# Delta rule's key-times-value product in the attention's rotating PSUM bank; first three second-layer weight casts of the feed-forward in traced order

## The chip, the cores and the metric

One core of one Trainium2 chip runs the kernel in one launch. The metric is device time in microseconds (us): the median of three timed runs of the kernel before is 1024.48 us (1024.39 to 1025.72).

## The reference

One layer of a hybrid encoder step, in float32, for two groups that share the weights: a prompt of 512 tokens and a sample of 64 tokens that has caches and a recurrent state. Width 1024, 4 heads in each attention, feed-forward width 4096.

```python
# h = x + W_out [ GDN_group(n) ; DiffAttn_group(n) ],  n = rmsnorm(x)
# h = h + MemCrossAttn(rmsnorm(h), memory K/V)
# h = h + W2 relu(W1 rmsnorm(h))^2
def step(S, xs):                                   # gated delta rule, one chunk
    u_c, w_c, qk_c, qg_c, kd_c, gl_c = xs
    vn = u_c - jnp.einsum('bhcd,bhde->bhce', w_c, S)
    o = jnp.einsum('bhcd,bhde->bhce', qg_c, S) + jnp.einsum('bhij,bhje->bhie', qk_c, vn)
    S = S * gl_c[..., None, None] + jnp.einsum('bhcd,bhce->bhde', kd_c, vn)
    return S, o
oa = _rmsnorm(oa, p['gdn_norm']) * jax.nn.silu(z)  # output of the delta rule, normalized and gated
h = h + jnp.square(jax.nn.relu(hn @ p['w_ff1'])) @ p['w_ff2']
```

The change touches the last product of `step`, kd times vn, that makes the next state, and the weights of `w_ff2`. The outputs include the new state of both groups.

## The kernel before

**Numbers.** Large products run in a split form: weight and activation are each cut into a high part (a cast on ScalarE, ACT) and a rest (a subtraction on VectorE, DVE), and three matmuls, high-high, high-low and low-high, add up in PSUM. In the program's names `wh`, `wl`, `w2h`, `w2l` are the parts of weights. The delta rule's own small products and transposes run on float32 tiles of 128 by 128.

**Stages.** Input projections come first (to about 120 us), then the gated delta rule over the prompt in four chunks of 128 tokens (to about 275 us), then the difference attention of four heads with the sample's delta rule woven in, the memory attention, and from about 600 us the feed-forward in eight groups of 512 hidden columns. Projections of later stages (tiles `pr`) are issued between the delta rule's steps and fill TensorE (PE) while the other engines work.

**One chunk of the delta rule.** `gdn_prep` (the triangle's solve by doubling, tiles `g`, products with `Dt`, `X`, `Y`, mask products `B` of L725) runs one chunk ahead of `gdn_scan` (L782). `gdn_scan` makes, in this order: keys times state; `vn` (L801); the output `bo`, which adds queries times state and KQ times `vn` in a PSUM bank; kd times `vn` in a bank of its own; the state update `next_state` (L760), for the first chunk a copy on ACT, later four instructions on DVE (L766, one per head); and then `normed` (L769) on `bo`: a square on ACT (L773), a reduction (L774), three small operations (L775, L776, L778) around a power on GpSimd (L208), and the scaling into `on` (L780). `on` is transposed on PE (L113) and gated (L814). `gdn_scan_sample` (L817) does the same for the sample, from a state that DMA loads (L877) into the buffer of the prompt's state, after that has been written out (L872).

**Banks.** PSUM's eight banks are handed out by tag: `BANKS = dict(pr=3, ba=2, g0=1, g1=1, gs=1)` (L75). A tag with one buffer makes each new tile wait until the last reader of the one before is done. All products of `gdn_scan` take "gs", one after the other. The tag "ba" turns over two buffers and serves the attention: transposes of keys and values (results copied at L932, L937, L940, and keys sent out at L938 and L941), and in the feed-forward the sums of `ff1_pair`. Tiles of one tag take their buffers in the order in which the program was written.

**Order.** Each engine runs its instructions in a fixed order. A scheduler sets it when the kernel is built, from dependences, the order in which the program was traced, and priorities: what is issued under `tc.high_priority()` is placed as early as it can be. DMAs of weights and states are issued on SP's queue, in order too.

**Feed-forward, the first split group.** `ff1_pair` makes two blocks of 128 hidden columns by seven products of twelve matmuls, numbered 1 to 7, in the order 1, 5, 6, 2, 7, 3, 4. `x`, `y`, `z` are the banks "ba", "gs" and "g1" that they add into; `keep` (L1364 to L1367, copy at L1366) saves the sum in a bank before the next product adds to it: product 6 adds to `x` after the first `keep`, product 7 after the third, product 3 to `z` after the second. `weights2` (L1334) loads a block of `w_ff2` (256 KB, DMA at L1336) and `split` casts it (L1330 on ACT, L1331 on DVE) with high priority. In the loop over groups g = 1 to 7 and blocks m = 0 to 7, `ff1_pair` runs at m = 0 and m = 4, and `project` with block m of the second layer at each m (L1519).

Of the kernel before, what the change touches and what calls it, by code (L numbers as in the profile page):

```python
# [15 lines left out]
P = 128  # L16
# [21 lines left out]
def hybrid_layer_kernel(  # L38
# [61 lines left out]
    def bank(tag="ba"):  # L100
        return ps.tile([P, 512], F32, tag=tag, name=nm(tag), bufs=BANKS[tag])
# [145 lines left out]
    w2 = w_in[0]  # L247
# [246 lines left out]
    for a0, n in HALVES:  # L494
        b = bank("pr")
# [286 lines left out]
    def gdn_scan(c, L, q, S):  # L782

        (_, kb), (cq, qb) = (blocks(typ, c, L) for typ in (1, 0))
        wide = [P, 4, P]

        def each(f):
            b = bank("gs")
            for h in range(H):
                f(b[:, h * P : (h + 1) * P], h)  # L790
            return v4(b, 4)

        if S is None:
            r = q["vb"]
        else:
            b = each(lambda o, h: mm(o, kb(h), S[:, h, :]))
            r = sb("r", 1)
            V.tensor_tensor(r, q["vb"], b, ALU.subtract)
        b = each(lambda o, h: mm(o, q["X"][:, h, :], r[:, h, :]))
        vn = sb("vn", 1)  # L800
        V.tensor_tensor(vn, b, q["brk"].unsqueeze(2).to_broadcast(wide), ALU.mult)  # L801

        def out(o, h):
            if S is not None:
                mm(o, qb(h), S[:, h, :], stop=False)
            mm(o, q["KQ"][:, h, :], vn[:, h, :], start=S is None)

        bo = each(out)
        b = each(lambda o, h: mm(o, q["kd"][:, h, :], vn[:, h, :]))
        S = next_state(c, S, b)  # L810
        on = sb("on", 1)
        normed(q, 4, [(slice(0, P), bo)], on)
        bt = each(lambda o, h: tr(o, on[:, h, :]))
        V.scalar_tensor_tensor(cq, bt, gn, zs[:, :, L], ALU.mult, ALU.mult)  # L814
        return S

    def gdn_scan_sample(q, S):  # L817
# [6 lines left out]
        def pairs(b):  # L824
            return b.rearrange("p (b i v) -> p b i v", b=2, i=2)

        def each(f, n=2 * P):
            b = bank("gs")
            for i in range(nb):
                f(b[:, i * n : (i + 1) * n], i)  # L830
            return b
# [17 lines left out]
            mm(o, q["KQ"][:, i, :], vw[:, i, :], start=False)  # L849

        bo = pairs(each(out))
        S = next_state(c, S, v4(each(lambda o, i: mm(o, q["kd"][:, i, :], vw[:, i, :])), 4))
        nc.sync.dma_start(o_gdn_s[0, 0].rearrange("h k v -> k h v"), S)
        yield
        on4 = sb("on", 1)
# [467 lines left out]
    odd = lambda: ft("f1", [P, 2, 4, T], 1, F32R)  # L1323
    rB = ft("rB", [P, T], 1)

    def split(src, tag, bufs, dma=False):
        shape = list(src.shape)
        wh, wl = (ft(tag + x, shape, bufs, F32R) for x in "hl")
        with tc.high_priority():
            A.copy(wh, src)  # L1330
            V.tensor_tensor(wl, src, wh.bitcast(F32), ALU.subtract)  # L1331
        return wh, wl

    def weights2(w, c0):  # L1334
        raw = ft("r2", [P, 4, P], 3)
        nc.sync.dma_start(raw, w[:, c0 : c0 + P].rearrange("(k p) n -> p k n", p=P))  # L1336
        return split(raw, "w2", 3)

    NG = 8

# [173 lines left out]
    for g in range(1, NG):  # L1514
        nxt = odd() if g % 2 else pair(5, F32R)
        for m in range(KT):
            if m % 4 == 0:
                ff1_pair(2 * g + m // 4, nxt)
            project(weights2(w_ff2[0, (g - 1) * 512 : g * 512, :], m * P), (pend,), add_group(g - 1, m), kt=4)  # L1519
            if g == 2:  # L1520
                with tc.issue_after(nc.cur_bb.bb.instructions[-1]):
                    square_block(m)
            if g == 3 and m == 0:
                norm_rows()
            if g == NG - 1:
                merge(V, m, slice(0, T if m < 4 else 256))
                if m >= 4:
                    last_weights(2 * m - 8)
        pend = nxt
# [57 lines left out]
```

## Time and profile before

| what | value |
|---|---|
| median of three timed runs | 1024.48 us (1024.39 to 1025.72) |
| profiled execution, its own time | 1023.02 us |
| its span in the trace | 1021.3 us |
| mean granted clock of TensorE | 0.998 |
| ScalarE busy | 535.1 us (52%) |
| HBM read and written | 88.88 MB, 87 GB/s over the span |

Times in the trace are microseconds from the span's start. A row of the timeline has the start, the time, the engine, the line of the kernel, the operation, the tile written and the tiles read, how many instructions the row joins, and in brackets the idle time before it with what ended it. PE is matmuls, PEld the weight loads that overlap them. A product of float32 tiles shows twice as many matmuls in the trace as the program issues.

### The profile page before, as it was taken

The page shows a single profiled execution, that of the slowest core. Times are in us where ns is not written, and L with a number is a line of the kernel's source. Part 1 is how long each engine was busy: PE and PEld are TensorE (multiplying, and loading weights), DVE is VectorE, ACT ScalarE, POOL GpSimd, SP SyncE. Part 2 cuts the span into 40 slices and gives each one's busy share as a digit, 9 for nine tenths or more (in the row PEclk, how much of TensorE's full clock was granted, in tenths as well). Part 3 has the DMA queues.
Part 4 walks back from the last instruction along what each step waited for, and adds up shares of the span by engine and source line. Part 5 has one row for each costly group of instructions (what it writes and reads, how often), then busy time and mean ns, then how long its engine had stood idle before and what let it go on. Part 6 is the DMA issues. An engine that isn't in the chain of part 4 may idle for free.

```text
span 1021.3 us, 17302 instructions
## 1 busy us (share of the span) xinstructions
PE 999.5 (98%) x6630; PEld 917.5 (90%) x6630; DVE 705.8 (69%) x1529; ACT 535.1 (52%) x1170; POOL 66.9 (7%) x131
## 2 busy tenths in 40 slices
PE   9999999999999999999999999999999999999986
PEld 7989899998888877899998998999999999999976
DVE  6666785776567676666666787757766677777893
ACT  6654664343364675544454657655545554555434
POOL 3441010100000000000000000000000000000030
PEclk9999999999999999999999999999999999999999
DMA  7432320100312255624121233422222222222102
GB/s 203 131 109 71 105 85 21 44 21 22 105 47 81 71 194 185 186 83 120 47 63 42 63 114 93 125 83 83 83 83 84 83 83 83 83 83 85 61 21 93
DMA packets 121254, 89.99 MB, mean 88 GB/s; under 512 B 5506, under 2 KB 112128, under 8 KB 120660
## 3 DMA queue, kind: packets, MB, share of 16 engines
q1 hardware_dynamic: 120804, 88.24, 29.4%
q8 instruction: 52, 0.85, 0.4%
q10 hardware_dynamic: 368, 0.66, 0.2%
q14 instruction: 30, 0.25, 0.1%
HBM read 79.14 MB, written 9.74 MB: 87 GB/s over the span
## 4 chain that ended last, share of the span: by engine, by line
PE 83%; DVE 5%; issue 3%; ACT 2%; POOL 2%; DMA 1%; POOLq 0%; ACTq 0%; DVEq 0%; SPq 0%
PE pr L107 48%; PE g L107 14%; PE ba L107 10%; PE gs L107 7%; PE ba L113 2%; PE g L113 2%; DVE u L1439 1%; DMA r<-in_w_ff_dram 1%; DVE wl L162 0%; POOL tg L208 0%; DMA S<-in_state_gdn_dram 0%; DVE p L457 0%; DMA out_dram<-S 0%; POOL X L604 0%; DVE on L780 0%
## 5 line engine op out<-in xcount | busy, mean ns | idle before, releaser
L107 PE MATMUL pr<-u,wh 128*128 128x320 f32 (+2 forms) x1240 | 326.9, 342 | 1.1 <-DVE p L323 1.0
L107 PE MATMUL pr<-u,wl 128*128 128x256 f32 (+1 forms) x816 | 228.3, 304 | 0.0
L107 PEld LDWEIGHTS pr<-u,wh 128*128 128x128 f32 x1240 | 211.4, 188 | 17.1 <-DVE p L323 1.3
L107 PEld LDWEIGHTS pr<-u,wl 128*128 128x128 f32 x816 | 149.9, 189 | 3.5 <-issue 0.7
L162 DVE TENSOR_TENSOR wl<-raw,wh 128x1024 fp32r<-128x1024 f32 x65 | 79.5, 1223 | 43.5 <-ACT wh L161 41.7
L161 ACT CAST wh<-raw 128x1024 fp32r<-128x1024 f32 x65 | 68.2, 1049 | 72.4 <-PE pr L107 55.5
L107 PE MATMUL pr<-u,w2h 128*128 128x320 f32 (+1 forms) x384 | 98.5, 340 | 1.4 <-DVE u L1415 0.7
L1330 ACT CAST w2h<-r 128x512 fp32r<-128x512 f32 x56 | 34.7, 620 | 92.3 <-PE pr L107 89.2
L107 PE MATMUL pr<-f,w2h 128*128 128x320 f32 (+1 forms) x288 | 73.8, 340 | 0.0
L107 PEld LDWEIGHTS pr<-u,w2h 128*128 128x128 f32 x384 | 65.0, 188 | 6.9 <-DVE u L1415 1.0
L107 PE MATMUL pr<-u,w2l 128*128 128x256 f32 (+1 forms) x256 | 65.2, 295 | 0.0
L107 PE MATMUL ba<-u,wl 128*128 128x288 f32 x360 | 53.0, 296 | 2.1 <-ACT keep L1366 2.1
L1415 DVE TENSOR_TENSOR u<-u,pr 128x256 f32<-128x256 f32 x96 | 42.9, 449 | 16.4 <-PE pr L107 15.6
L107 PEld LDWEIGHTS pr<-f,w2h 128*128 128x128 f32 x288 | 48.7, 188 | 4.2 <-issue 1.2
L107 PEld LDWEIGHTS ba<-u,wl 128*128 128x128 f32 x360 | 49.2, 188 | 3.0 <-ACT keep L1366 3.0
L107 PE MATMUL pr<-f,w2l 128*128 128x256 f32 (+1 forms) x192 | 48.8, 295 | 0.0
L107 PEld LDWEIGHTS pr<-u,w2l 128*128 128x128 f32 x256 | 46.9, 188 | 1.5
L1331 DVE TENSOR_TENSOR w2l<-r,w2h 128x512 fp32r<-128x512 f32 x56 | 39.2, 701 | 11.7 <-ACT w2h L1330 11.4
L107 PE MATMUL pr<-wh,u 128*128 128x512 f32 x128 | 41.2, 401 | 0.0
L1423 POOL TENSOR_TENSOR u<-u,rB 128x320 f32<-128x320 f32 x4 | 3.7, 921 | 497.4 <-ACT u L1438 492.8
L107 PEld LDWEIGHTS pr<-f,w2l 128*128 128x128 f32 x192 | 35.2, 188 | 1.1
L1375 ACT ACTIVATE c<-c 128x288 f32<-128x288 f32 x48 | 21.0, 442 | 28.5 <-DVE c L1374 28.5
(505 smaller groups left out, 2091.5 us busy)
## 6 DMA issues: line engine op xcount, KB each, us to landing
raw<-in_w_ff_dram SPq DMA_DIRECT2D x36, 512.0 KB
raw<-in_w_in_dram SPq DMA_DIRECT2D x28, 512.0 KB
r<-in_w_ff_dram SPq DMA_DIRECT2D x56, 256.0 KB
raw<-in_w_mem_k_dram SPq DMA_DIRECT2D x8, 512.0 KB
raw<-in_w_mem_v_dram SPq DMA_DIRECT2D x8, 512.0 KB
raw<-in_w_out_dram SPq DMA_DIRECT2D x8, 512.0 KB
raw<-in_w_mem_q_dram SPq DMA_DIRECT2D x8, 512.0 KB
raw<-in_w_mem_o_dram SPq DMA_DIRECT2D x8, 512.0 KB
```

The costliest lines, as they stand in the source:

```text
L107: i = nc.tensor.matmul(out, lhsT, rhs, start=start, stop=stop, skip_group_check=skip_group_check)
L113: i = nc.tensor.transpose(out, in_, ident[:n, :n])
L161: A.copy(wh, raw)
L162: V.tensor_tensor(wl, raw, wh.bitcast(F32), ALU.subtract)
L1330: A.copy(wh, src)
L1331: V.tensor_tensor(wl, src, wh.bitcast(F32), ALU.subtract)
L1375: A.activation(c, c, AF.Relu)
L1415: V.tensor_tensor(am, am, b, ALU.add)
L1423: eng.tensor_tensor(am, am, rB[:, n], ALU.mult)
L1439: V.tensor_tensor(lo, src, hi.bitcast(F32), ALU.subtract)
```

## The change

The inner function `each` of both scans takes the tag of its bank. Only kd times `vn` is given another, "ba" in place of "gs"; what is computed stays the same. In the feed-forward `split` and `weights2` take a flag `urgent` in place of an unused one; the casts of the blocks m = 0, 1, 2 of group g = 1 are issued without high priority, all others as before.

```diff
--- before.py
+++ after.py
@@ -784,8 +784,8 @@
         (_, kb), (cq, qb) = (blocks(typ, c, L) for typ in (1, 0))
         wide = [P, 4, P]
 
-        def each(f):
-            b = bank("gs")
+        def each(f, tag="gs"):
+            b = bank(tag)
             for h in range(H):
                 f(b[:, h * P : (h + 1) * P], h)
             return v4(b, 4)
@@ -806,7 +806,7 @@
             mm(o, q["KQ"][:, h, :], vn[:, h, :], start=S is None)
 
         bo = each(out)
-        b = each(lambda o, h: mm(o, q["kd"][:, h, :], vn[:, h, :]))
+        b = each(lambda o, h: mm(o, q["kd"][:, h, :], vn[:, h, :]), "ba")
         S = next_state(c, S, b)
         on = sb("on", 1)
         normed(q, 4, [(slice(0, P), bo)], on)
@@ -824,8 +824,8 @@
         def pairs(b):
             return b.rearrange("p (b i v) -> p b i v", b=2, i=2)
 
-        def each(f, n=2 * P):
-            b = bank("gs")
+        def each(f, n=2 * P, tag="gs"):
+            b = bank(tag)
             for i in range(nb):
                 f(b[:, i * n : (i + 1) * n], i)
             return b
@@ -849,7 +849,7 @@
             mm(o, q["KQ"][:, i, :], vw[:, i, :], start=False)
 
         bo = pairs(each(out))
-        S = next_state(c, S, v4(each(lambda o, i: mm(o, q["kd"][:, i, :], vw[:, i, :])), 4))
+        S = next_state(c, S, v4(each(lambda o, i: mm(o, q["kd"][:, i, :], vw[:, i, :]), tag="ba"), 4))
         nc.sync.dma_start(o_gdn_s[0, 0].rearrange("h k v -> k h v"), S)
         yield
         on4 = sb("on", 1)
@@ -1323,18 +1323,18 @@
     odd = lambda: ft("f1", [P, 2, 4, T], 1, F32R)
     rB = ft("rB", [P, T], 1)
 
-    def split(src, tag, bufs, dma=False):
+    def split(src, tag, bufs, urgent):
         shape = list(src.shape)
         wh, wl = (ft(tag + x, shape, bufs, F32R) for x in "hl")
-        with tc.high_priority():
+        with tc.high_priority() if urgent else ExitStack():
             A.copy(wh, src)
             V.tensor_tensor(wl, src, wh.bitcast(F32), ALU.subtract)
         return wh, wl
 
-    def weights2(w, c0):
+    def weights2(w, c0, urgent):
         raw = ft("r2", [P, 4, P], 3)
         nc.sync.dma_start(raw, w[:, c0 : c0 + P].rearrange("(k p) n -> p k n", p=P))
-        return split(raw, "w2", 3)
+        return split(raw, "w2", 3, urgent)
 
     NG = 8
 
@@ -1516,7 +1516,7 @@
         for m in range(KT):
             if m % 4 == 0:
                 ff1_pair(2 * g + m // 4, nxt)
-            project(weights2(w_ff2[0, (g - 1) * 512 : g * 512, :], m * P), (pend,), add_group(g - 1, m), kt=4)
+            project(weights2(w_ff2[0, (g - 1) * 512 : g * 512, :], m * P, g > 1 or m > 2), (pend,), add_group(g - 1, m), kt=4)
             if g == 2:
                 with tc.issue_after(nc.cur_bb.bb.instructions[-1]):
                     square_block(m)
```

The products stay as many as before; the order on the engines is another, from the first chunk of the delta rule to the end of the difference attention, and again in the first feed-forward group.

First place: TensorE in the third chunk (chunk 2), from the last matmul of the output `bo` (tile `gs_2438`) on. `vn_2436` times `kd_1987` is the product in question, `on_2456` the normalized output, `g_...` the next chunk's triangle, `pr_...` a projection. Before:

```order
L107 MATMUL gs_2438<-vn_2436,KQ_2031 128x128
L113 MATMUL g_392_2342<-ident,Dt_380_2296 128x128 x4
L113 MATMUL g_423_2474<-ident,u_75 128x128 x2
L107 MATMUL pr_3089<-u_94,wh_3064 128x320 x2
L107 MATMUL pr_3089<-u_94,wl_3065 128x320 x2
L107 MATMUL g_395_2351<-Dt_380_2296,B_394_2349 128x128 x4
L107 MATMUL pr_3089<-u_94,wh_3064 128x320 x2
L107 MATMUL pr_3122<-u_93,wh_3118 128x512
L107 MATMUL pr_3122<-u_93,wl_3119 128x256
L107 MATMUL gs_2447<-vn_2436,kd_1987 128x128
L107 MATMUL g_396_2357<-Y_393_2348,X_2295 128x128 x4
L107 MATMUL gs_2447<-vn_2436,kd_1987 128x128 x3
```

And now, from the row after the output's last matmul:

```order
L113 MATMUL g_392_2342<-ident,Dt_380_2296 128x128 x4
L107 MATMUL ba_2447<-vn_2436,kd_1987 128x128 x4
L107 MATMUL g_395_2351<-Dt_380_2296,B_394_2349 128x128 x4
L113 MATMUL g_423_2474<-ident,u_75 128x128 x2
L107 MATMUL pr_3068<-u_94,wh_3064 128x512
L107 MATMUL pr_3068<-u_94,wl_3065 128x256 x2
L107 MATMUL g_396_2357<-Y_393_2348,X_2295 128x128 x4
L107 MATMUL pr_3068<-u_94,wh_3064 128x512
L107 MATMUL pr_3089<-u_93,wh_3064 128x320 x2
L113 MATMUL g_426_2482<-ident,u_78 128x128 x2
L107 MATMUL pr_3089<-u_93,wl_3065 128x320
L113 MATMUL gs_2466<-ident,on_2456 128x128 x4
```

The product stands right behind the output in a "ba" tile, and the transposes of `on` stand about where the product stood.

The same chunk on VectorE, from the reduction L774 to the scaling L780 and behind it. Before:

```order
L774 TENSOR_REDUCE tg_2457<-on_2456 128x4
L775 TENSOR_TENSOR tg_2457<-tg_2457,tg_2035 128x4
L776 TENSOR_SCALAR tg_2457<-tg_2457 128x4
L778 TENSOR_TENSOR tg_2458<-tg_2458,tg_1980 128x4
L780 TENSOR_TENSOR on_2456<-gs_2438,tg_2458 128x512
L725 SCALAR_TENSOR_TENSOR B_404_2391<-lev,At_371_2267 128x512
L918 COPY qz_2680<-pr_3089 64x320
L162 TENSOR_TENSOR wl_3185<-raw_3182,wh_3184 128x1024
L741 TENSOR_TENSOR Dt_380_2296<-Dt_380_2296,g_396_2357 128x512
L766 SCALAR_TENSOR_TENSOR S_1962<-S_1962,egl,gs_2447 128x128 x4
```

And now:

```order
L774 TENSOR_REDUCE tg_2457<-on_2456 128x4
L775 TENSOR_TENSOR tg_2457<-tg_2457,tg_2035 128x4
L766 SCALAR_TENSOR_TENSOR S_1962<-S_1962,egl,ba_2447 128x128 x3
L725 SCALAR_TENSOR_TENSOR B_404_2391<-lev,At_371_2267 128x512
L766 SCALAR_TENSOR_TENSOR S_1962<-S_1962,egl,ba_2447 128x128
L776 TENSOR_SCALAR tg_2457<-tg_2457 128x4
L678 TENSOR_TENSOR kd_2477<-g_423_2474,kdc_1194 128x256
L778 TENSOR_TENSOR tg_2458<-tg_2458,tg_1980 128x4
L780 TENSOR_TENSOR on_2456<-gs_2438,tg_2458 128x512
```

The four updates of the state (L766), a mask product (L725) and a scaling of the prepared keys (L678) moved ahead of the normalization's last steps.

Second place: TensorE in the fourth chunk. `u_78` holds keys of the attention's first head, whose transposes go to "ba" tiles. Before, around kd times `vn`:

```order
L107 MATMUL gs_2628<-vn_2617,kd_2233 128x128 x3
L107 MATMUL g_462_2586<-Y_459_2579,X_2525 128x128 x2
L107 MATMUL gs_2628<-vn_2617,kd_2233 128x128
L107 MATMUL pr_3188<-u_93,wl_3185 128x256
L107 MATMUL pr_3188<-u_94,wh_3184 128x512
L107 MATMUL pr_3188<-u_94,wl_3185 128x256
L113 MATMUL g_463_2590<-ident,Dt_441_2526 128x128 x2
L107 MATMUL pr_3188<-u_94,wh_3184 128x512
L107 MATMUL pr_3188<-u_94,wl_3185 128x256
L107 MATMUL pr_3188<-u_94,wh_3184 128x512
L107 MATMUL g_466_2597<-Dt_441_2526,B_465_2595 128x128 x2
L113 MATMUL gs_2647<-ident,on_2637 128x128 x4
```

And now, from that product on:

```order
L107 MATMUL ba_2628<-vn_2617,kd_2233 128x128 x2
L107 MATMUL g_461_2582<-Dt_441_2526,B_460_2580 128x128 x2
L107 MATMUL ba_2628<-vn_2617,kd_2233 128x128 x2
L113 MATMUL ba_2765<-ident,u_78 128x128
L107 MATMUL g_462_2586<-Y_459_2579,X_2525 128x128 x2
L113 MATMUL ba_2765<-ident,u_78 128x128
L107 MATMUL pr_3122<-u_94,wl_3119 128x256
L107 MATMUL pr_3122<-u_94,wh_3118 128x512
L107 MATMUL pr_3147<-u_93,wh_3118 128x320
L113 MATMUL ba_2797<-ident,u_78 128x128
L113 MATMUL g_463_2590<-ident,Dt_441_2526 128x128 x2
L113 MATMUL ba_2797<-ident,u_78 128x128
```

The product moved ahead, next to the triangle's products, and the transposes of the first head's keys (`ba_2765`, `ba_2797`) moved behind it; they had been issued in earlier chunks. SP's queue, with the write of the prompt's state (L872) and the load of the sample's (L877), before:

```order
L157 DMA raw_3807<-in_w_in_dram 128x8x128
L872 DMA out_dram<-S_1962 128x4x128
L1140 DMA B_926_5048<-in_cache_mem_v_dram 128x512
L949 DMA u_76<-in_cache_diff_v_dram 128x2x512
L877 DMA S_2663<-in_state_gdn_dram 128x4x128
```

And now:

```order
L938 DMA out_dram<-p_493_2768 128x2x128
L872 DMA out_dram<-S_1962 128x4x128
L938 DMA out_dram<-p_496_2801 128x2x128
L941 DMA out_dram<-p_496_2801 64x128
L951 DMA p_509_2880<-in_cache_diff_k_dram 128x512
L877 DMA S_2663<-in_state_gdn_dram 128x4x128
```

Three transfers of the attention (L938, L941, L951) stand between the write and the load, in place of two (L1140, L949).

Third place: ScalarE in the first split pair of feed-forward group 1. `keep_6776`, `keep_6790` and `keep_6804` are the three copies, `w2h_7084` and `w2h_7115` second-layer blocks. Before:

```order
L1229 CAST wh_6881<-raw_6757 128x512
L1330 CAST w2h_7084<-r_1263_7082 128x512
L1380 CAST u_6616<-c_6730 128x288
L1330 CAST w2h_7115<-r_1268_7113 128x512
L1229 CAST wh_6884<-s_1225_6879 128x512
L1366 COPY keep_6776<-ba_6761 128x288
L1366 COPY keep_6790<-g_1216_6763 128x288
L1366 COPY keep_6804<-ba_6761 128x288
L1375 ACTIVATE c_6818<-c_6818 128x288
```

And now:

```order
L1229 CAST wh_6881<-raw_6757 128x512
L1380 CAST u_6616<-c_6730 128x288
L1366 COPY keep_6776<-ba_6761 128x288
L1330 CAST w2h_7084<-r_1263_7082 128x512
L1229 CAST wh_6884<-s_1225_6879 128x512
L1366 COPY keep_6790<-g_1216_6763 128x288
L1330 CAST w2h_7115<-r_1268_7113 128x512
L1366 COPY keep_6804<-ba_6761 128x288
L1375 ACTIVATE c_6818<-c_6818 128x288
```

Each cast of a second-layer block moved back behind a `keep` that it stood ahead of.

## The prediction

> **What bounds the kernel now.** I read the page's busy shares first, then the list of waits of TensorE (PE), then stretches of 25 us, then the timeline at the two places that the diff touches.
>
> ```profile
> span 1021.3 us, 17302 instructions
> PE 999.5 (98%) x6630; PEld 917.5 (90%) x6630; DVE 705.8 (69%) x1529; ACT 535.1 (52%) x1170; POOL 66.9 (7%) x131
> ```
>
> PE is busy for 999.5 of 1021.3 us, so only some 22 us of idle exist, start and tail included. An edit that leaves PE's work alone, as this one does, gains or loses through PE's waits. Those that bear on the change (engine, tile and line, what was waited for; us in total, times, longest):
>
> ```profile
> PE gs L107 <- DVE on L780: 2.1, 4, 0.9
> PE ba L107 <- ACT keep L1366: 2.1, 1, 2.1
> PE gs L107 <- DMA S<-in_state_gdn_dram: 0.5, 1, 0.5
> ```
>
> The first is the product kd·vn waiting for the one "gs" bank, which the normalization of the output (L780) still reads. The second is the sixth of the seven products of a pair in the first split feed-forward group. The third is the sample's state, loaded over DMA into the buffer that the prompt's state had.
>
> ```profile
> 225.00:250.00 25.00, 23.97 (x189) 21.59 (x189) 13.90 (x34) 9.10 (x19) 2.02 (x2) 1.00 0.09 22
> 250.00:275.00 25.00, 24.66 (x185) 21.77 (x185) 16.17 (x40) 9.37 (x21) 1.01 (x1) 1.00 0.25 68
> 650.00:675.00 25.00, 24.97 (x171) 23.86 (x170) 14.94 (x26) 16.39 (x39) 0.00 (x0) 1.00 0.31 91
> ```
>
> The columns are length, then busy us of PE, PEld, DVE, ACT, POOL, the granted clock, DMA. In the delta rule (first two rows) PE still has a microsecond of idle; in the feed-forward (third) it has none, so a microsecond won just before that stage is kept to the end, with nothing behind to take it back.
>
> **Part B, the casts.** PE and then ACT in the pair concerned:
>
> ```profile
> 622.92 1.75 PE L107 MATMUL g<-u,wh 128*128 128x288 f32 x12
> 624.51 1.61 PE L107 MATMUL gs<-u,w 128*128 128x288 f32 x11
> 628.22 1.86 PE L107 MATMUL ba<-u,wl 128*128 128x288 f32 x12 [2.10 <-ACT keep L1366]
> 633.72 1.87 PE L107 MATMUL ba<-u,w 128*128 128x288 f32 x12
> ```
> ```profile
> 623.25 0.60 ACT L1229 CAST wh<-raw 128x512 fp32r<-128x512 f32 x1
> 625.86 0.62 ACT L1330 CAST w2h<-r 128x512 fp32r<-128x512 f32 x1 [2.01 <-DMA r<-in_w_ff_dram]
> 626.38 0.42 ACT L1380 CAST u<-c 128x288 fp32r<-128x288 f32 x1
> 626.73 0.62 ACT L1330 CAST w2h<-r 128x512 fp32r<-128x512 f32 x1
> 627.25 0.61 ACT L1229 CAST wh<-s 128x512 fp32r<-128x512 f32 x1
> 627.77 0.39 ACT L1366 COPY keep<-ba 128x288 f32<-128x288 f32 x1
> 628.06 0.40 ACT L1366 COPY keep<-g 128x288 f32<-128x288 f32 x1
> ```
>
> The in-order ScalarE stands at the cast of a second-layer block whose DMA has not landed (2.01 us idle), and the copy `keep` that frees product 6's bank is queued behind it. Twelve matmuls take 624.51 − 622.92 = 1.59 us, 0.1325 each. The trace has 49 matmuls from 624.51 to 633.72: 6.5 us of work in 9.2, so 2.7 us are lost here, 2.1 of them in the listed wait.
>
> Afterwards the first `keep` stands ahead of that cast: behind the `wh` cast (ends 623.85), `u` (0.35 by the step 626.38 to 626.73) and 0.3 for itself it is done at about 624.5, as PE comes to product 6. The cast still begins when its block lands, 625.86; behind it come 0.52 (it), 0.52 (`wh`), 0.29 (second `keep`), 0.52 (second block's cast) and 0.39 (third `keep`): 628.1. PE runs products 6 and 2, 24 × 0.1325 = 3.2 us, from 624.6 to 627.8 and waits 0.3 for the third `keep`. Then 25 matmuls, 3.3 us, lead to the product now at 633.72: it starts at 631.4. I take **−2.2 us**; −2.7 would need no wait at all; −1.7 if the second block lands half a microsecond later than its cast shows. The third block's cast comes later still, and its consumer is a whole pair away.
>
> **Part A, the waits at kd.** The four waits sum to 2.1 us, and each goes, since "ba" has two buffers and stands free there: −2.1. What matters is where PE meets the same chain next: the transposes of `on`, which need the normalization anyway. Chunk 2, PE and then VectorE (DVE):
>
> ```profile
> 235.94 0.66 PE L113 MATMUL g<-ident,Dt 128*128 128x128 f32 x4
> 236.43 0.38 PE L113 MATMUL g<-ident,u 128*128 128x128 f32 x2
> 237.32 1.16 PE L107 MATMUL g<-Dt,B 128*128 128x128 f32 x8
> 238.24 0.77 PE L107 MATMUL pr<-u,wh 128*128 128x320 f32 x3
> 240.01 0.49 PE L107 MATMUL gs<-vn,kd 128*128 128x128 f32 x2 [0.88 <-DVE on L780]
> 240.33 1.06 PE L107 MATMUL g<-Y,X 128*128 128x128 f32 x8
> 241.22 0.83 PE L107 MATMUL gs<-vn,kd 128*128 128x128 f32 x6
> ```
> ```profile
> 237.64 0.17 DVE L776 TENSOR_SCALAR tg<-tg 128x4 f32<-128x4 f32 x1
> 239.26 0.69 DVE L780 TENSOR_TENSOR on<-gs,tg 128x512 f32<-128x512 f32 x1
> 239.87 0.68 DVE L725 SCALAR_TENSOR_TENSOR B<-lev,At 128x512 f32<-128x512 f32 x1
> 242.60 1.11 DVE L766 SCALAR_TENSOR_TENSOR S<-S,egl,gs 128x128 f32<-128x128 f32 x4
> ```
>
> From the output's last matmul (the next row starts at 235.94) to the end of L780 (239.95) the chain takes 4.0 us. In the new order the four state updates (1.11) and one mask product B (0.6) stand on DVE ahead of L776: 5.6 us. PE has ahead of the transposes, in the new order, the transposes of Dt (0.49), kd (eight at about 0.12, 0.9), two groups of eight at 0.9 and some 1.5 of short transposes and projections: 4.7. The wait comes back at the same 0.9. Chunk 0's wait (0.2) returns too, for its state is copied by ACT and the chain stays as it is; in chunk 1 there are 35 rows of PE work between, and I take 0. Bounds: each of the three can return nothing, or at most its present wait and the 1.8 us of DVE work put ahead. Sum +1.1, between 0 and 6.
>
> **Part A, chunk 3 and the state's load.** PE, then the DMA queue of SP:
>
> ```profile
> 263.20 0.39 PE L107 MATMUL gs<-vn,KQ 128*128 128x128 f32 x2
> 268.26 0.94 PE L107 MATMUL gs<-vn,kd 128*128 128x128 f32 x6 [0.26 <-DVE on L780]
> 269.48 0.39 PE L107 MATMUL gs<-vn,kd 128*128 128x128 f32 x2
> 274.25 0.46 PE L107 MATMUL pr<-u,wh 128*128 128x320 f32 x2
> 274.69 0.46 PE L107 MATMUL pr<-u,wh 128*128 128x320 f32 x2
> 278.48 1.10 PE L107 MATMUL gs<-S,KQ 128*128 128x256 f32 x4 [0.54 <-DMA S<-in_state_gdn_dram]
> ```
> ```profile
> 271.17 0.39 SPq L872 DMA_DIRECT2D out_dram<-S  x1
> 274.58 0.37 SPq L877 DMA_DIRECT2D S<-in_state_gdn_dram  x1
> ```
>
> The chain is kd, state update, write of the state (271.17), load of the sample's state into its buffer (274.58), first use (278.48): 7.3 us from write to use. In the new order kd follows the output at once, so the chain starts sooner, but PE reaches the use sooner still: two projections stand behind the use that stood ahead of it. After the output: kd and two products of the triangle, 1.9 us; transposes of keys and values of head 0, which now come third in the two "ba" buffers and wait for kd's update. ACT's square, the reduction (0.7), L775, the update in two halves around one mask step of 0.4: done at about 3.2 us, where PE arrives at 2.5. The write goes out at 3.2, the use at 3.2 + 7.3 = 10.5. PE's own work up to there: 1.9, then 2.8 of transposes and triangle products with the transposes of `on`, then 22 matmuls of 320 columns at 0.147 (three in 274.69 − 274.25): 3.2; with a few short ones 8.1. So PE waits 2.4 in this stretch, where before it waited 0.26 (already removed above) and 0.54: **+1.9**. It is −0.5 if enough projections still cover it, and at most +2.6 with another 0.7 for the three small issues now ahead of the load on SP (0.37 each, two of them inside the 3.4 us from write to load). The sample's own kd wait (0.8, the rest of the 2.1) does not return: its transposes come some 85 rows of PE later.
>
> PE's filler is shuffled over some 580 rows; the shuffle alone I put at 0, ±2.
>
> By a page, "DMA: Bandwidth & Descriptors" of the Trainium skill (§ Anatomy of one DMA), a transfer has a fixed part of about 2.0 us and bytes over 436 GB/s: estimated, 2.6 us for the 256 KB of state. The trace has 3.9 from issue to use, so by the page alone this last wait would be 1.3 shorter and the sum below −2.6.
>
> **Sum**: −2.2 − 2.1 + 1.1 + 1.9 = −1.3 us. The profiled execution took 1023.02 (its span and 1.7 around it), 1.5 under the median shown: it would read 1021.7, and the median 1024.48 − 1.3 = **1023.2**.
>
> **The rivals.** About 0.2%, 2 us, is what a measurement can tell from no change.
>
> First, *the waits do not return*: chunk 3's load stays covered and the transposes find their input ready, both terms near 0.3 together: −4.0, 1020.5. For it: the rows of filler between kd and the transposes. A further gain would come from weight loads: in the two delta-rule windows PEld is busy 43.4 us, against 2 × 23.86 = 47.7 in the feed-forward, so PE's busy time hides some 4.4 us of slack; half of it recovered gives 1018.3. In a sentence beside it: the Trainium skill, "Perfetto Trace Analysis" (§ Identifying the Most-Contended Engine), holds matmul busy time a poor measure of headroom and the weight-load share a good one; these rows agree that the 98% overstates how full PE is. Against it: the orders put DVE work ahead of the norm and take filler from ahead of the load.
>
> Second, *slower: the norm late on DVE in every chunk*. The engine runs in order, and state update, mask product and a key scaling (L678) stand ahead of L776 with GpSimd's power behind it; PE then stands at the transposes in each of chunks 0 to 2, up to 1.9 us each (0.1 above the added 1.8), and 2.6 at the load: 5.7 + 2.6 − 4.3 = +4.0, 1028.5. It decides from (2 + 4.3 − 1.9) / 3 = 1.5 us per chunk. For it: DVE has 5.6 us to do and PE 4.7 in chunk 2. Against: chunk 1's long cover, and chunk 0, where ACT makes the state.
>
> Third, *B does not do what it says*: the block lands late enough that the third `keep` stalls product 7 as long as the first did product 6. Then −2.2 goes: 1025.4. Against: 24 matmuls now stand between.
>
> **How the numbers follow.** The forecast 0.45 (own range 1021 to 1025.5: faster 0.12, same 0.31, slower 0.02), the waits that stay away 0.27 (faster 0.26, same 0.01), the late norm 0.22 (slower), B without effect 0.06 (same 0.05, slower 0.01). Faster 0.38, same 0.37, slower 0.25. The range 1019.8 to 1027.4 leaves out the weight-load gain and the late norm at its full price.
>
> **What would show it.** B: the wait of "ba" on `keep` gone from the list, a wait of at most 0.5 at product 7, and the stretch of 49 matmuls from 9.2 to about 7.0 us. A: no wait of kd on L780; in its place one of "gs" transposes on L780 of about 0.9 in chunk 2 and under 0.3 in chunks 0 and 1; a wait of "ba" on the update L766 of some 0.7; a wait on the state's DMA of 1 to 2 us. I am wrong if that DMA wait is gone, if the transposes wait over 1.5 us in three chunks, or if PE loses time at a place named nowhere here.

## The result, and the profile after

| | before | changed |
|---|---|---|
| median of 22 runs each, us | 1024.74 (1022.59 to 1027.13) | 1023.23 (1022.00 to 1024.16) |
| ratio, 95% interval | | 0.9984 (0.9978 to 0.9991) |
| profiled execution, its own time and span, us | 1023.02, 1021.3 | 1022.98, 1021.3 |

The kernel became faster by 0.16%, 1.6 us (0.9 to 2.3). That is less than the 2 us that the prediction took for what a measurement can tell from no change, but 22 runs tell it. The two profiled executions, however, took the same time, so the page alone does not show where the gain is. Part of the answer is the granted clock of the single executions, which the experiments below take up. The page after, first rows:

```profile
span 1021.3 us, 17300 instructions
PE 1000.5 (98%) x6630; PEld 917.8 (90%) x6630; DVE 706.3 (69%) x1529; ACT 534.6 (52%) x1170; POOL 67.7 (7%) x131
```

The waits of PE after the change that answer to the three shown of before (what waits, for what; us in total, times, longest):

```profile
PE ba L107 <- ACT keep L1366: 1.2, 1, 1.2
...
PE gs L107 <- DVE on L780: 0.7, 1, 0.7
PE gs L113 <- DVE on L780: 0.7, 2, 0.4
PE g L107 <- ACT B L715: 0.6, 1, 0.6
```

None of these four is a wait of kd. The row "gs L107" on L780 is now a product of the attention (below), "gs L113" are the transposes of `on`, and L715 belongs to the next chunk's preparation. The wait on the state's load is gone from this execution.

The feed-forward pair, PE after the change:

```profile
625.29 1.86 PE L107 MATMUL ba<-u,wl 128*128 128x288 f32 x12
626.99 1.74 PE L107 MATMUL gs<-u,w 128*128 128x288 f32 x12
629.93 1.85 PE L107 MATMUL ba<-u,wl 128*128 128x288 f32 x12 [1.20 <-ACT keep L1366]
```

And ScalarE there:

```profile
624.85 0.39 ACT L1366 COPY keep<-ba 128x288 f32<-128x288 f32 x1
627.62 0.62 ACT L1330 CAST w2h<-r 128x512 fp32r<-128x512 f32 x1 [2.38 <-DMA r<-in_w_ff_dram]
628.15 0.61 ACT L1229 CAST wh<-s 128x512 fp32r<-128x512 f32 x1
628.67 0.39 ACT L1366 COPY keep<-g 128x288 f32<-128x288 f32 x1
628.96 0.62 ACT L1330 CAST w2h<-r 128x512 fp32r<-128x512 f32 x1
629.48 0.40 ACT L1366 COPY keep<-ba 128x288 f32<-128x288 f32 x1
```

Product 6 starts at 625.29 without a wait; the first `keep` stands ahead of the block's cast, as the order says. But in this execution the block's cast had to wait for its DMA until 627.62, so the third `keep` is late and product 7 waits 1.20 us. From the end of product 5 to the start of product 4, the prediction's stretch of 49 matmuls, it is 8.1 us (625.29 to 633.38), where it was 9.2 and was to be about 7.0.

Chunk 2 after the change, PE from the output's end on and then the VectorE operations that answer to those shown of before:

```profile
233.48 0.66 PE L113 MATMUL g<-ident,Dt 128*128 128x128 f32 x4
233.97 1.06 PE L107 MATMUL ba<-vn,kd 128*128 128x128 f32 x8
...
239.22 0.66 PE L113 MATMUL gs<-ident,on 128*128 128x128 f32 x4 [0.41 <-DVE on L780]
```
```profile
235.07 0.86 DVE L766 SCALAR_TENSOR_TENSOR S<-S,egl,ba 128x128 f32<-128x128 f32 x3
236.06 0.69 DVE L725 SCALAR_TENSOR_TENSOR B<-lev,At 128x512 f32<-128x512 f32 x1
236.67 0.34 DVE L766 SCALAR_TENSOR_TENSOR S<-S,egl,ba 128x128 f32<-128x128 f32 x1
236.93 0.16 DVE L776 TENSOR_SCALAR tg<-tg 128x4 f32<-128x4 f32 x1
...
238.47 0.69 DVE L780 TENSOR_TENSOR on<-gs,tg 128x512 f32<-128x512 f32 x1
```

kd runs at once; the updates stand ahead of L776, and `on` is ready 5.7 us after the output (233.48 to 239.16), where it took 4.0 before. The state's way, PE and SP:

```profile
271.72 1.02 PE L107 MATMUL gs<-S,KQ 128*128 128x256 f32 x4
```
```profile
265.45 0.45 SPq L872 DMA_DIRECT2D out_dram<-S  x1
...
268.02 0.38 SPq L877 DMA_DIRECT2D S<-in_state_gdn_dram  x1
```

The first use follows the write's issue by 6.3 us (7.3 before), and without a listed wait.

To split the difference by stage I compare the start of the same matmul in both traces: the 1051st (end of the part that is alike), the 4000th from the end (a memory projection), the 2600th from the end (in product 5 of the feed-forward pair) and the 2400th from the end (a second-layer projection), at 162.6, 402.5, 623.5 and 654.5 us in the trace of before. In the tables below, "delta rule and attention" is the time from the first to the second of them, and "feed-forward pair" from the third to the fourth. Before they took 239.92 and 31.04, after 240.60 and 30.44: in these two executions the bank change cost 0.7 us and the casts gave 0.6.

### The profile page after: what moved, and what is told of

It is laid out like the page before. It is cut to its first block, busy times and chain, and to the rows that moved or that the text cites. A ratio compares the mean times of both kernels' runs of the same rounds, so it can differ in the third digit from the quotient of the medians.

```text
span 1021.3 us, 17300 instructions
## 1 busy us (share of the span) xinstructions
PE 1000.5 (98%) x6630; PEld 917.8 (90%) x6630; DVE 706.3 (69%) x1529; ACT 534.6 (52%) x1170; POOL 67.7 (7%) x131
## 4 chain that ended last, share of the span: by engine, by line
PE 63%; DVE 2%; issue 2%; ACT 1%; DMA 1%; POOL 0%; POOLq 0%; ACTq 0%; SPq 0%
PE pr L107 39%; PE ba L107 10%; PE g L107 8%; PE gs L107 4%; PE ba L113 2%; DVE u L1439 1%; DMA r<-in_w_ff_dram 1%; DMA raw<-in_w_ff_dram 0%; DVE u L1423 0%; DVE u L1415 0%; ACT c L1376 0%; ACT c L1375 0%; DVE u L1424 0%; ACT u L1467 0%; DVE u L1417 0%
## 5 line engine op out<-in xcount | busy, mean ns | idle before, releaser
L107 PE MATMUL pr<-u,wh 128*128 128x320 f32 (+2 forms) x1240 | 327.1, 342 | 1.4 <-DVE p L323 1.0
L107 PE MATMUL pr<-u,wl 128*128 128x256 f32 (+1 forms) x816 | 227.8, 303 | 0.0
L107 PEld LDWEIGHTS pr<-u,wh 128*128 128x128 f32 x1240 | 211.7, 188 | 17.0 <-DVE p L323 1.3
L107 PEld LDWEIGHTS pr<-u,wl 128*128 128x128 f32 x816 | 150.1, 189 | 3.6 <-issue 0.7
L107 PE MATMUL pr<-u,w2h 128*128 128x320 f32 (+1 forms) x384 | 98.5, 340 | 1.4 <-DVE u L1415 0.7
L107 PE MATMUL pr<-f,w2h 128*128 128x320 f32 (+1 forms) x288 | 73.9, 340 | 0.0
L107 PEld LDWEIGHTS pr<-u,w2h 128*128 128x128 f32 x384 | 65.0, 188 | 6.7 <-DVE u L1415 1.0
L107 PE MATMUL pr<-u,w2l 128*128 128x256 f32 (+1 forms) x256 | 65.2, 295 | 0.0
L107 PE MATMUL ba<-u,wl 128*128 128x288 f32 x360 | 53.0, 296 | 1.3 <-ACT keep L1366 1.2
L107 PEld LDWEIGHTS pr<-f,w2h 128*128 128x128 f32 x288 | 48.7, 188 | 4.0 <-issue 1.1
L107 PEld LDWEIGHTS ba<-u,wl 128*128 128x128 f32 x360 | 49.2, 188 | 2.0 <-ACT keep L1366 1.9
L107 PE MATMUL pr<-f,w2l 128*128 128x256 f32 (+1 forms) x192 | 48.9, 295 | 0.0
L107 PEld LDWEIGHTS pr<-u,w2l 128*128 128x128 f32 x256 | 46.9, 188 | 1.5
L107 PE MATMUL pr<-wh,u 128*128 128x512 f32 x128 | 41.4, 400 | 0.0
L107 PEld LDWEIGHTS pr<-f,w2l 128*128 128x128 f32 x192 | 35.2, 188 | 1.1
```

Of the source, the lines that this page charges most:

```text
L107: i = nc.tensor.matmul(out, lhsT, rhs, start=start, stop=stop, skip_group_check=skip_group_check)
```

## The experiments

Twelve kernels, each timed against the kernel before in five rounds and profiled once. They ran in four sets on different chips: e1 to e4, e5 to e8, e9 to e11, and e12. The median of before in them is 1025.29, 1024.81, 1025.91 and 1024.82 us, so medians of different sets compare only roughly; the ratios are taken within a set.

**The parts alone, and both kernels again.** The casts alone (e1) leave the bank as it was:

```diff
-        b = each(lambda o, h: mm(o, q["kd"][:, h, :], vn[:, h, :]), "ba")
+        b = each(lambda o, h: mm(o, q["kd"][:, h, :], vn[:, h, :]))
...
-        S = next_state(c, S, v4(each(lambda o, i: mm(o, q["kd"][:, i, :], vw[:, i, :]), tag="ba"), 4))
+        S = next_state(c, S, v4(each(lambda o, i: mm(o, q["kd"][:, i, :], vw[:, i, :])), 4))
```

> Casts in traced order, the bank as before. Theory 1 (the gain is the casts', the bank change nets about nothing): 1.0 to 2.0 us faster than before, ratio 0.998 to 0.999, a wait of product 7 on keep of about 1 us in place of the 2.1 us of product 6. Theory 2 (the gain is the bank's): within 0.5 us of before.

The bank alone (e2) makes the casts urgent again:

```diff
-            project(weights2(w_ff2[0, (g - 1) * 512 : g * 512, :], m * P, g > 1 or m > 2), (pend,), add_group(g - 1, m), kt=4)
+            project(weights2(w_ff2[0, (g - 1) * 512 : g * 512, :], m * P, True), (pend,), add_group(g - 1, m), kt=4)
```

> The bank changed, the casts urgent as before. Theory 1: within 0.8 us of before, rather above than below; in the profile the feed-forward begins some 0.7 us later than in the profile of before. Theory 2: 1.0 to 1.6 us faster. The wait of product 6 on keep (2.1 us before) stays under both.

The two kernels unchanged:

> The kernel before, unchanged, for a second profile. Theory 3 (the first profile of before, 1.7 us under the median of its runs, was a quick execution and the median execution waits longer for a DMA): the execution profiled here has a longer wait on keep or on the state's load than 2.1 and 0.5 us, if its time is nearer the median. Rival: the waits are the same and the time differs in the launch around the span. Ratio 1.000 within 0.0007.

> The changed kernel, unchanged, for a second profile. Theory 3: the waits on DMA (block of the second layer, 2.4 us idle of ScalarE in the first profile; state load covered) move by several tenths of a us from run to run, but the wait on keep that PE sees stays under 1.5 us. Ratio to before 0.998 to 0.999.

| kernel | median (range), us | ratio to before, interval | profiled, us | delta rule and attention | feed-forward pair |
|---|---|---|---|---|---|
| e1 casts only | 1022.47 (1021.16 to 1024.62) | 0.9980 (0.9969 to 0.9990) | 1022.54 | 239.98 | 30.19 |
| e2 bank only | 1025.43 (1024.00 to 1027.00) | 1.0006 (0.9994 to 1.0017) | 1025.05 | 241.46 | 31.12 |
| e3 before again | 1024.75 (1023.06 to 1027.77) | 1.0002 (0.9990 to 1.0013) | 1023.06 | 239.98 | 30.61 |
| e4 after again | 1023.38 (1022.25 to 1025.37) | 0.9986 (0.9974 to 0.9997) | 1024.47 | 241.75 | 29.63 |

Theory 1 holds: the gain is the casts' (2.0 us, 1.0 to 3.2), and the bank change nets nothing that the runs can tell (0.6 us slower, from 0.6 faster to 1.7 slower). In the three traces that have the bank change the delta rule and attention take 240.6 to 241.8 us, in the three that don't 239.9 to 240.0: there it costs every time. Its delay at the feed-forward is larger in e2 (2.1 us, 1.5 of them in this stretch) than the 0.7 that was expected.

Theory 3 was not borne out: the second profile of before was again a short execution (1023.06), with 1.7 us on `keep` and 0.6 on the state, against medians of 1024.7 and 1025.3. So no trace shows what the longer executions of before wait for.

Their granted clock tells them apart, however. Of the 98 runs of before beside the twelve kernels, 75 have a mean granted clock of TensorE of 0.993 to 0.996, and the other 23 have 0.997 or 0.998; in each set the 75 are longer, by 1.5 to 2.7 us in the mean. Of 34 runs of the changed kernel (the 22 and e4's 12) none is under 0.997; of e1's 12 two are, of e2's 12 eight. Two profiles, e9 and e11 (below), caught such a fall in the feed-forward pair: the granted clock is 0.5 for 3.41 us, from 632.53 and from 631.34. Product 7 had waited for `keep` there for 1.75 and 1.91 us, to 631.28 and 630.87. In e9 its twelve matmuls then take 2.25 us, where they took 1.85 after:

```profile
631.28 2.25 PE L107 MATMUL ba<-u,wl 128*128 128x288 f32 x12 [1.75 <-ACT keep L1366]
```

Half of 3.41 is 1.7 us, an estimate of what one such fall costs; over 1024 us it lowers the mean clock by 0.0017, about the step between the two groups. Three executions of before in four at 1.7 us make 1.3 us, so by this estimate most of the 1.6 us is that executions of the changed kernel keep their clock; what the casts save beside that, the bank change nearly takes back, as the equal spans of the two profiles have it. Among the runs at 0.997 and more there is no gain to see: before has medians of 1022.8 to 1024.5 by set, the changed kernel 1023.2 (the 22) and 1023.4 (e4). But those runs of before may be the ones whose waits were short. What decides whether a wait is followed by a fall was not worked out: in the profiles of before, e2 and e3, product 6 waits 1.7 to 2.2 us and the clock stays.

What differs between the profiled executions in this pair is when the block lands. SP's rows for the loads of second-layer blocks (five joined in each; m=1 is the first of them), before and in e4:

```profile
619.85 8.95 SPq L1336 DMA_DIRECT2D r<-in_w_ff_dram  x5
```
```profile
622.92 9.32 SPq L1336 DMA_DIRECT2D r<-in_w_ff_dram  x5
```

And the cast that waits for it, in e4 and in e9 (the state's buffer, below; its load is issued at 621.40):

```profile
629.16 0.62 ACT L1330 CAST w2h<-r 128x512 fp32r<-128x512 f32 x1 [1.61 <-DMA r<-in_w_ff_dram]
```
```profile
628.98 0.62 ACT L1330 CAST w2h<-r 128x512 fp32r<-128x512 f32 x1 [2.95 <-DMA r<-in_w_ff_dram]
```

From issue to cast that is 6.0 us before, 6.2 in e4 and 7.6 in e9; the ten traces in which two transfers of 512 KB stand ahead of the block have 5.5 (e8) to 7.7 (e11).

**Loading the block earlier.** e5 keeps everything of before, the urgent casts too, and writes the loads of the first three blocks ahead of the first-layer loads of the next pair; on SP the block m=1 then stands ahead of one of the two transfers of 512 KB. e6 is the same with the casts of e1.

```diff
+    for m in range(3):
+        early[1, m] = load2(1, m)
     ff1_pair(1, pend)
```

> Bank and casts as before (casts urgent); the second-layer block m=1 is loaded ahead of 512 KB of the next pair's weights, m=2 behind them. Theory 1 (product 6 waits because ScalarE stands at a block that has not landed): the block's cast waits some 1.5 us less for its DMA, the wait of product 6 on keep falls from 2.1 and 1.7 us to 0.2 to 0.7, and the time falls by about as much as with the casts alone in traced order, 1.0 to 2.5 us. Rival (the casts' own place in the queue costs it, two times 0.5 us, landed or not): the wait stays above 1.0 and the time falls by less than 1 us.

> Bank as before, casts in traced order, and the block m=1 loaded earlier as in the run beside it. Theory 1: product 7 waits under 0.4 us for keep (0.7 with the casts alone), 2 to 3 us faster than before. Rival (earlier landing is worth nothing more once the first keep is out of its way): as fast as the casts alone within 0.3 us.

| kernel | median (range), us | ratio to before, interval | profiled, us | delta rule and attention | feed-forward pair |
|---|---|---|---|---|---|
| e5 blocks first | 1021.82 (1021.16 to 1022.35) | 0.9971 (0.9962 to 0.9980) | 1021.65 | 239.99 | 29.44 |
| e6 casts and blocks | 1021.31 (1020.48 to 1021.54) | 0.9969 (0.9958 to 0.9980) | 1021.54 | 240.16 | 29.12 |

In e5, PE and then ScalarE:

```profile
625.31 1.87 PE L107 MATMUL ba<-u,wl 128*128 128x288 f32 x12 [0.19 <-ACT keep L1371]
628.93 1.85 PE L107 MATMUL ba<-u,wl 128*128 128x288 f32 x12 [0.17 <-ACT keep L1371]
```
```profile
622.86 0.62 ACT L1330 CAST w2h<-r 128x512 fp32r<-128x512 f32 x1 [0.18 <-DMA r<-in_w_ff_dram]
```

(L1371 is the same `keep`, five lines on.) With the cast still urgent, the block lands 3 us sooner and the wait of product 6 falls from 2.10 to 0.19 us. The order on ScalarE moved too (the second block's cast and one of a first-layer weight now stand behind the first `keep`, at 626.81 and 627.34), so e5 alone does not separate the two. The rows of before do: of the 2.10 us that product 6 waited, ScalarE stood idle at the block for 2.01. So it is the late block that held product 6, not the casts' place by itself, and the rival falls. The spread of the timed runs shrinks with it, from 3.9 us (30 runs of before beside it) to 1.2, and none of the 11 runs has a clock under 0.997, where 24 of those 30 do. That is the best evidence that the longer executions of before lose their time at this block, by a longer wait and a fall of the clock behind it; no trace of before shows one. Early loads and traced order hardly add up: e6 lies 0.5 us under e5 with overlapping intervals; two ways out of one wait.

**Which part of the bank change costs.** e7 is the full change without the sample's tag; e8 sends the chunks' product to the triangle's bank of the same parity:

```diff
-        b = each(lambda o, h: mm(o, q["kd"][:, h, :], vn[:, h, :]), "ba")
+        b = each(lambda o, h: mm(o, q["kd"][:, h, :], vn[:, h, :]), f"g{c % 2}")
```

> Casts in traced order; the bank changed in the prompt's chunks only, the sample's product back on gs. Theory A1 (each wait at kd comes back at the next reader, so nothing is won by the sample's part): within 0.4 us of the full change, the wait on L780 at the sample's kd again 0.7 to 0.9. Theory A2 (the cost sits in the sample's part and the attention around it): faster than the full change by 0.8 us or more, near the casts alone.

> Casts in traced order; the chunks' kd product goes to the triangle's bank of its own parity, g0 or g1, which is idle then, instead of ba, so that the attention's transposes keep their order; the sample's on gs. Theory A3 (the bank change costs because it pushes head 0's transposes and the projections into another order): 0.5 to 1.5 us faster than the full change, at or below the casts alone. Theory A1 (the chain through the norm sets the time whatever bank kd takes): within 0.5 us of the casts alone, the waits at kd replaced by waits at the transposes of on.

| kernel | median (range), us | ratio to before, interval | profiled, us | delta rule and attention | feed-forward pair |
|---|---|---|---|---|---|
| e7 chunks only | 1023.26 (1021.71 to 1025.11) | 0.9990 (0.9981 to 0.9998) | 1022.00 | 240.47 | 29.40 |
| e8 triangle bank | 1022.94 (1021.86 to 1024.64) | 0.9988 (0.9979 to 0.9996) | 1021.86 | 240.51 | 28.95 |

Both times equal the full change within their intervals. The sample's part is the clear one. With its tag (the full change) and without it (e7), the one wait on L780 that stands at the sample:

```profile
308.34 0.68 PE L107 MATMUL gs<-u,aT 128*128 128x128 f32 x4 [0.69 <-DVE on L780]
```
```profile
PE gs L107 <- DVE on L780: 0.9, 1, 0.9
```

kd no longer waits for "gs" (0.79 before), and the next product that wants "gs", the attention's, waits 0.69 for the very same release. Theory A1 holds there. In e8 the attention's transposes stay in the early chunks, as before the change, and the stretch is no shorter (240.51 against 240.60), so theory A3 falls: the waits only go elsewhere, 0.67 us at a transpose for L680, 0.85 for L715, 0.20 at `on`.

**The state's buffer.** e9 is the full change, e10 is e6, both with the sample's state in the buffer `Y1` of the preparation, so that its load no longer waits for the write of the prompt's state:

```diff
-    S = sb("S")
+    S = sb("Y1")
     nc.sync.dma_start(S, state_gdn[0, 0].rearrange("h k v -> k h v"))
```

> The full change, with the sample's state loaded into a buffer of the triangle's preparation that is free by then, ahead of the write of the prompt's state. Theory B1 (the wait of PE at the sample's first product, 0, 0.9 and 1.2 us in three profiles with the bank change, is the late state, whatever name stands beside it): that wait is gone in every profile, the stretch from 163 to 403 us takes about 240.5 us where it took 240.6 to 241.8, and the time falls by 0.4 to 1.2 us against the full change. Rival B2 (the named VectorE operations L202 and L924 hold it): the wait stays.

> Bank as before; casts in traced order, the block m=1 loaded ahead, and the sample's state in a buffer of its own. Theory B1: 0.5 to 0.8 us faster than without the state's buffer (its wait of 0.5 to 0.8 us is gone), some 4 us under before. Rival: the 0.7 comes back a few products later, same within 0.3.

e11 is the full change with `normed` written ahead of the kd product and the update:

```diff
+        normed(q, 4, [(slice(0, P), bo)], on)
         b = each(lambda o, h: mm(o, q["kd"][:, h, :], vn[:, h, :]), "ba")
         S = next_state(c, S, b)
-        on = sb("on", 1)
-        normed(q, 4, [(slice(0, P), bo)], on)
```

> The full change with the normalization written ahead of the kd product and the state update, so that VectorE does the norm first. Theory C1 (what the bank change costs in the chunks is the state update ahead of the norm on VectorE): the two waits at the transposes of on (0.3 and 0.4) vanish and the stretch from 163 to 403 us shrinks by 0.5 to 0.8 us. Rival C2 (it is the next chunk's preparation left without cover, as at L715, and the changed mix of small products): the stretch stays within 0.4 us, or grows because the state comes later.

e12 is e10 with the bank change of chunks and sample on top:

> The kernel with casts in traced order, block m=1 loaded ahead and the state in a buffer of its own, and on top of it the bank change in chunks and sample; both waits that hang on a DMA are out of the way. Theory A (the bank change costs by itself, through the order that it makes): the stretch from 163 to 403 us takes about 240.8 us as with the own state and the bank change, against 239.2 without it, and the time is 1 to 1.8 us above that kernel's 1021.0. Rival (its cost was only the late state): within 0.4 us of that kernel.

| kernel | median (range), us | ratio to before, interval | profiled, us | delta rule and attention | feed-forward pair |
|---|---|---|---|---|---|
| e9 own state | 1024.08 (1023.49 to 1025.91) | 0.9987 (0.9977 to 0.9996) | 1025.70 | 240.84 | 32.12 |
| e10 all fixes | 1021.01 (1020.33 to 1021.67) | 0.9952 (0.9939 to 0.9964) | 1021.01 | 239.18 | 28.93 |
| e11 norm first | 1022.66 (1021.45 to 1025.33) | 0.9966 (0.9954 to 0.9977) | 1025.33 | 240.66 | 32.54 |
| e12 bank on fixes | 1022.76 (1021.84 to 1023.21) | 0.9974 (0.9964 to 0.9983) | 1023.15 | 240.84 | 29.21 |

The first product on the sample's state in e2, e4 and e11, in this order:

```profile
273.27 1.10 PE L107 MATMUL gs<-S,KQ 128*128 128x256 f32 x4 [0.88 <-DVE u L202]
```
```profile
273.33 1.10 PE L107 MATMUL gs<-S,KQ 128*128 128x256 f32 x4 [1.16 <-DVE u L924]
```
```profile
271.76 1.10 PE L107 MATMUL gs<-S,KQ 128*128 128x256 f32 x4 [1.06 <-DMA S<-in_state_gdn_dram]
```

With the own buffer no wait there is listed in any of e9, e10 and e12, as theory B1 has it: the operations of VectorE named in the first two rows were not what held it. From e6 to e10 the stretch falls from 240.16 to 239.18. The timed runs leave the size open: the medians, of different sets, differ by 0.3 us, under the 0.5 to 0.8 that was expected, and the ratios by 1.7, with intervals that overlap. e9's time did not fall (ratio 0.9987, the full change 0.9984): its profile has a late block instead, the wait that the casts alone leave open, and behind it the fall of the clock (32.12 in the pair).

e11 keeps waits at the transposes of `on` (1.0 us in three), and the stretch is 240.66. In chunk 2, PE and VectorE:

```profile
232.04 0.66 PE L113 MATMUL g<-ident,Dt 128*128 128x128 f32 x4
...
236.92 0.66 PE L113 MATMUL gs<-ident,on 128*128 128x128 f32 x4 [0.44 <-DVE on L780]
```
```profile
236.18 0.68 DVE L780 TENSOR_TENSOR on<-gs,tg 128x512 f32<-128x512 f32 x1
```

`on` is ready 4.8 us after the output instead of 5.7, but the scheduler now puts 4.4 us of PE's work ahead of the transposes (236.92 − 0.44 − 232.04) where it had 5.3, so the wait is the same, against C1. But the equal stretch does not speak for C2. It has 1.06 us of wait on the state in it, and the full change's first profile has none. Without that wait the stretch is 239.6 us in e11, 240.6 in both profiles of the full change and in e2, and 239.3 to 239.4 in before, e1, e3, e5 and e6. So with the normalization first some 1.0 us comes back (one profile), and here the state's load takes it away again. The wait at L715 is gone in e11 too. That may be why its ratio is better than the full change's by 0.0018, beside intervals of 0.0011 to each side and from another set; it is not shown, since its profiled execution is a long one (a late block and a fall of the clock, 32.54 in the pair).

e12 settles the bank change. With both waits on DMA out of the way it costs 1.66 us in the trace (240.84 against 239.18), and 1.75 us in the medians, whose ranges (1020.33 to 1021.67 and 1021.84 to 1023.21) don't meet, though the two ran on different chips; the ratios, 0.9952 and 0.9974, touch at the ends of their intervals. No run of either has a clock under 0.997. The waits that are listed by name nearly cancel: e10 has 2.1 us at kd, e12 in their place

```profile
PE gs L107 <- DVE on L780: 0.9, 1, 0.9
...
PE gs L113 <- DVE on L780: 0.7, 2, 0.4
PE g L107 <- ACT B L715: 0.6, 1, 0.6
```

which is 2.2 (2.1 when the single waits are added). The 1.6 us lie in no wait that the list has: the same 1580 matmuls stand in another order. Outside the listed waits the stretch takes 235.8 us in e10, 237.4 in e12 and in the first profile of the full change, and 236.2 in e11 with the normalization first. Nearly all of it is in the products into `g` tiles (L107; the triangle's and the attention's, 497 matmuls in the stretch): counted from each start to the next, listed waits left out, they take 64.2 us in e10, 65.8 in e12 and 64.5 in e11. Why they take longer in that order was not settled.

e10, without the bank change, is the fastest kernel: 0.9952 (0.9939 to 0.9964), 4.9 us under the runs of before beside it, and 2.9 under those of them that have a clock of 0.997 and more.

## Why the prediction was right, point by point

The time came out (1023.2 forecast, 1023.23 measured), and in the timed runs each of its two halves nearly so: casts −2.2 forecast and −2.0 in e1, bank +0.9 forecast (−2.1 + 1.1 + 1.9) and +0.6 in e2, +1.7 in e12. But the sum was worked out from the waits of a trace, and in the traces it did not come. The profiled execution was to read 1021.7 us; it read 1022.98, and 1024.47 in e4, where before has 1023.02 and 1023.06. What the medians gained is, by the estimate above, mostly the clock that executions of before lose, a term that the sum does not have. The premise that an edit which leaves PE's work alone gains or loses through PE's listed waits failed twice: at the clock, and at the 1.6 us of e12 that no listed wait holds. So the direction and the places were foreseen, and the agreement to 0.03 us is luck.

- **The casts.** Right in mechanism: the first `keep` no longer stands behind the block's cast, and product 6 no longer waits. The size was too large for the traces: the stretch of 49 matmuls takes 9.2, 9.3 and 8.8 us in before, e2 and e3, and 8.1, 7.7 and 7.3 in after, e1 and e4, 1.4 less on average and not 2.2 (to which the prediction rounds a working that gives 2.3, 633.72 to 631.4). The 2.0 of e1's timed runs has the clock in it. The third `keep` behind the block's cast was foreseen; its wait of 0.3 was mis-sized, because it took the landing of one execution. It was 1.2 after, 0.7 in e1, 0.4 in e4 and 1.8 in e9. The third rival (the late block stalls product 7 as it did product 6) is therefore not an alternative but what happens in part of the executions.
- **kd's waits.** Gone wherever kd has another bank, as said.
- **The transposes of `on`.** Forecast 0.2, 0 and 0.9, measured 0.27, 0 and 0.41 in chunks 0 to 2. The chain was foreseen to a tenth (5.6 us forecast, where 4.0, 1.1 and 0.6 make 5.7; 5.7 measured); PE's work ahead of the transposes was under-counted, 4.7 against 5.3 us (239.22 − 0.41 − 233.48).
- **The state's load.** Forecast +1.9. Against 0.5 to 0.6 before, the first use waited 0 in the profile after, 0.9 in e2 and 1.2 in e4: mechanism right, term too large. PE was to reach the use 2.4 us early and to wait 0.7 of it at the first head's transposes; no wait on L766 is listed at all, and in the profile after, the use starts 6.3 us after the write's issue (265.45 to 271.72), not 7.3. The prediction counted the absence of this wait as a sign of being wrong: it is absent in the profile after, and e2 and e4 have it. The 2.6 us of the Trainium skill ("DMA: Bandwidth & Descriptors", § Anatomy of one DMA) comes from a fit that is stated there for transfers that GpSimd starts; this one is on SP's queue and took 3.7 us from issue to use (268.02 to 271.72), so the row, and not the page, was the right measure.
- **The sample.** Wrong: "does not return". The step looked 85 rows on to the sample's own transposes, but the bank passes in between to a product of the attention, and 0.69 of 0.79 us returned there.
- **The next chunk's preparation.** Not foreseen: 0.6 us at L715. The prediction counted time lost at a place that it did not name as a sign of being wrong, and this one came. Its cause is not shown; with the normalization first (e11) it is gone.
- **The shuffle.** Taken as 0 with 2 either way; e12 against e10 puts it at about +1.6, and e11 at less with the normalization first. This and the two missing waits (at the sample and at L715) are what the oversized state term stood in for.

The rival of the waits that stay away, and with it the gain from the slack of the weight loads, did not come: e10 wins without the bank change. The slower rival, 1.5 us and more at each chunk's transposes, is refuted by waits of 0.27 and 0.41.

## What to carry to other kernels

When a product gets another bank, follow the old bank to whoever takes it next, not to the next product of the same step: the release it waited for has not moved. The Trainium skill ("Perfetto Trace Analysis", § Matmuls) would have independent groups of matmuls rotate through different PSUM banks; here the rotation removed each wait it was aimed at and cost 1.7 us (e12), as the order of everything else moved with it. And where an in-order engine stands at a load, see what stands ahead of that load on its queue before moving the engine's work: 256 KB moved ahead of 512 KB (e5) gave at least as much as the casts' new place (ratios 0.9971 and 0.9980, overlapping intervals), and steadier times. And before a difference of 2 us is put down to waits, compare the granted clock of the runs on both sides.

## What the runs showed of the hardware

The same load of 256 KB, behind the same 1 MB of others, took from 5.5 to 7.7 us from its issue to the cast that reads it, over ten traces; behind half of that at most 4.3 (e5, e6, e10, e12). One profile cannot give a wait that hangs on it: the same code with traced-order casts showed 0.4 and 1.2 us at product 7. A wait of TensorE can cost more than its length: behind 1.75 and 1.91 us at product 7 (e9, e11) the granted clock was 0.5 for 3.41 us, while 2.10 us at product 6 in before left it at full. Both profiled executions of before (1023.02 and 1023.06, clocks 0.998 and 0.997) lay 1.7 us under the medians beside them (1024.74 and 1024.75), so two equal spans hid a change of 1.6 us that the timed runs show.
